# Sums over the partitions taken by GpSimd in place of matmuls of ones, and inverse roots computed on VectorE in place of GpSimd

## The chip, the cores and the metric

The kernel runs on one core of a Trainium2 chip. The metric is device time in microseconds (us) of one execution, as the median of several runs. The engines of the core are TensorE (PE, with its weight loads shown apart as PEld), VectorE (DVE), ScalarE (ACT), GpSimd (POOL) and SyncE (SP), which issues the loads and stores. Each takes its instructions in order and waits on semaphores that others raise.

## The reference, cut to what matters

```python
def rmsnorm(x, g):                       # mean over the 1024 columns
    return x * rsqrt(mean(x * x) + 1e-6) * g

def adaln(x, g, shift, scale):
    return rmsnorm(x, g) * (1 + scale[:, None, :]) + shift[:, None, :]

c_act = silu(c)                          # (1, 1024)
for i in range(2):
    mod = (c_act @ mod_w[i] + mod_b[i]).reshape(B, 3, 3, 1024)   # (shift, scale, gate) of 3 sublayers
    h = adaln(x, norm_g[i, 0], mod[:, 0, 0], mod[:, 0, 1])
    x = x + 0.5 * mod[:, 0, 2] * swiglu(h, ffn_w_in[i, 0], ffn_w_out[i, 0])
    h = adaln(x, norm_g[i, 1], mod[:, 1, 0], mod[:, 1, 1])
    x = x + mod[:, 1, 2] * (gmlp_mixer(h) if i == 0 else moba_mixer(h))
    h = adaln(x, norm_g[i, 2], mod[:, 2, 0], mod[:, 2, 1])
    x = x + 0.5 * mod[:, 2, 2] * swiglu(h, ffn_w_in[i, 1], ffn_w_out[i, 1])
return rmsnorm(x, final_norm)
```

x has 256 rows of 1024 columns, in float32. The feed-forward layers are 2816 wide. Each of the six sublayers needs three modulation vectors of 1024 columns: shift (part 0), scale (part 1) and gate (part 2), 18 vectors in all, each a product of one row with a 1024 x 1024 matrix. gmlp has a further rmsnorm, of its v half.

## The kernel before, in words

x stays in two tiles of 128 rows (t = 0, 1). All large products go through `gemm` (L201): the weights are loaded in tiles of 128 rows of the contraction, two to a transfer (`raw`, three buffers); each is split into a rounded part and a remainder, by ScalarE (L179) and VectorE (L180), into a slot `hl` (eight slots); and three TensorE products of the parts (high by high, high by low, low by high) are added up for each t. The slots set how far ScalarE and VectorE run ahead of TensorE.

The modulation vectors are prepared in the background, one stage ahead. `mod_unit(i, s, part)` stands for one vector: it clears a 128x1024 tile `ma` on GpSimd (L103), SP loads the bias row into its first row (L104), and four pieces each load two rows per partition of the weights (`mw`, L112, 1 MB) and add them, times the entries of c, with two VectorE instructions (L114). What is then left is a sum over the 128 partitions, which `reduce` takes. `gemm` calls the next of these small pieces at every fourth tile of weights (`tick`; every tile or every second one in moba). Units run for 16 of the 18 vectors; the first two (shift and scale of the first sublayer) are computed in `head` in another way.

`reduce` splits the accumulator into a rounded part and a remainder in a slot of `hl` (L121 on ScalarE, L122 on VectorE), multiplies both from the left by a matrix of ones on TensorE (L132; of halves for the gates that carry the factor 0.5), four matmuls for a vector, and copies the sums, which then stand in every row, from PSUM to `bc` (L137 on ScalarE; for the scale L134 on VectorE, which adds 1 and multiplies by the norm's weights).

At the end of a sublayer `residual` adds the gated result to x (L304, L305) and `ada` prepares the next sublayer's input: x times the scale vector (L290), the row's mean square (L264 on ScalarE, L268 on VectorE), its inverse root (`inverse_root`, L273: a power of -0.5 on GpSimd), and root and shift applied (L295), then transposes (L280) and another split (L282, L283). This is done for t = 0 while TensorE still computes t = 1, and for t = 1 while TensorE begins the next product with t = 0. `inverse_root` is called 16 times: twice in `head`, ten times in `ada`, twice for gmlp's v (`rv`), twice at the end. The tile framework places the instructions in each engine's order from its own plan of their times, so that the order on an engine is not quite that of the code.

Of the kernel before, what the change touches and what calls it, by code (L numbers as in the profile page):

```python
# [10 lines left out]

F32 = mybir.dt.float32
F32R = mybir.dt.float32r
AF = mybir.ActivationFunctionType
ALU = mybir.AluOpType
AX = mybir.AxisListType
# [2 lines left out]
P = 128  # L19
D = 1024  # L20
# [35 lines left out]
def trunk(ctx: ExitStack, tc: tile.TileContext, x, c, rel_bias, mod_w, mod_b, norm_g,  # L56
          ffn_w_in, ffn_w_out, gmlp_w_in, gmlp_v_norm, gmlp_w_s, gmlp_b_s, gmlp_w_out,
          moba_w_qkv, moba_w_o, final_norm, onehot, out):
    nc = tc.nc
    const = ctx.enter_context(tc.tile_pool(name="const", bufs=1))  # L60
    pool = ctx.enter_context(tc.tile_pool(name="pool", bufs=2))
# [4 lines left out]
    def acc_bank(name):  # L66
        return psum.tile([P, 512], F32, tag="acc", name=name, bufs=6)

    def tr_bank(name):
        return psum.tile([P, 512], F32, tag="tr", name=name, bufs=2)  # L70

    def hl_slot(shape, dt, name):
        return pool.tile(shape, dt, tag="hl", name=name, bufs=8)

    def small(name, w=1):
        return stat.tile([P, w], F32, tag=f"st{w}", name=name)

    def half_tile(name):
        return pool.tile([P, 512], F32, tag="half", name=name, bufs=4)

    x_sb = [const.tile([P, D], F32, name=f"x{t}") for t in range(NT)]
# [3 lines left out]
    make_identity(nc, ident)  # L85
    ones = const.tile([P, P], F32R, name="ones")
    nc.gpsimd.memset(ones.bitcast(F32), 1.0)
    halves_ = const.tile([P, P], F32R, name="halves")
    nc.gpsimd.memset(halves_.bitcast(F32), 0.5)
    mhalf = const.tile([P, 1], F32, name="mhalf")  # L90
    nc.gpsimd.memset(mhalf, -0.5)
    nc.scalar.activation(cs, cs, AF.Silu)


    def mod_unit(i, s, part):

        col = (s * 3 + part) * D
        st = {}
        src = mod_w[i].rearrange("(p k) n -> p k n", k=KD)

        def start():
            a = pool.tile([P, D], F32, tag="macc", name=f"ma{i}{s}{part}", bufs=2)
            nc.gpsimd.memset(a, 0.0)  # L103
            nc.sync.dma_start(a[0:1, :], mod_b[i:i + 1, col:col + D])  # L104
            st["acc"] = a

        def piece(k0):
            def f():
                if k0 == 0:
                    start()  # L110
                w = pool.tile([P, 2, D], F32, tag="mraw", name=f"mw{i}{s}{part}{k0}", bufs=2)
                nc.sync.dma_start(w, src[:, k0:k0 + 2, col:col + D])  # L112
                for j in range(2):
                    nc.vector.scalar_tensor_tensor(  # L114
                        st["acc"], w[:, j, :], cs[:, k0 + j:k0 + j + 1], st["acc"],
                        op0=ALU.mult, op1=ALU.add)
            return f

        def reduce():
            hl = hl_slot([P, 2, D], F32R, f"mhl{i}{s}{part}")  # L120
            nc.scalar.copy(hl[:, 0, :], st["acc"])  # L121
            nc.vector.tensor_sub(hl[:, 1, :], st["acc"], hl[:, 0, :].bitcast(F32))  # L122
            if part == 1:
                g = pool.tile([P, 2, D], F32, tag="mraw", name=f"g{i}{s}", bufs=2)
                nc.sync.dma_start(g[:, 0, :], norm_g[i, s:s + 1, :].to_broadcast([P, D]))
            bc = pool.tile([P, D], F32, tag="bc", name=f"bc{i}{s}{part}", bufs=3)
            lhs = halves_ if part == 2 and s != 1 else ones
            for h in range(2):
                ps = tr_bank(f"mps{i}{s}{part}{h}")
                sl = slice(h * 512, h * 512 + 512)  # L130
                for j in range(2):
                    nc.tensor.matmul(ps, lhs, hl[:, j, sl], start=j == 0, stop=j == 1)  # L132
                if part == 1:
                    nc.vector.scalar_tensor_tensor(bc[:, sl], ps, 1.0, g[:, 0, sl],  # L134
                                                   op0=ALU.add, op1=ALU.mult)
                else:
                    nc.scalar.copy(bc[:, sl], ps)  # L137
            vec[i, s, part] = bc

        return [piece(k) for k in range(0, KD, 2)] + [reduce]  # L140
# [13 lines left out]
    def split_weights(src, key, kt, cols):  # L154
# [22 lines left out]
        r = raws[key]  # L177
        hl = hl_slot([P, 2, D], F32R, f"hl_{key}_{kt}")
        nc.scalar.copy(hl[:, 0, :w], r[:, kt % 2, :w])  # L179
# [74 lines left out]
    def new_hT():  # L254
        hT["hi"] = pool.tile([P, KD, S], F32R, tag="hTh", name="hTh", bufs=1)
        hT["lo"] = pool.tile([P, KD, S], F32R, tag="hTl", name="hTl", bufs=1)

    def row_rstd(t, name):

        ss = []  # L260
        for h in range(2):
            a = small(f"ss{name}{h}")
            junk = half_tile(f"junk{name}{h}")
            nc.scalar.activation(junk, x_sb[t][:, h * 512:(h + 1) * 512], AF.Square,  # L264
                                 scale=1.0 / 32.0, accum_out=a)
            ss.append(a)
        m = small(f"m{name}")
        nc.vector.scalar_tensor_tensor(m, ss[0], EPS, ss[1], op0=ALU.add, op1=ALU.add)  # L268
        return inverse_root(m, name)

    def inverse_root(m, name):
        r = small(f"r{name}")
        nc.gpsimd.tensor_tensor(r, m, mhalf, op=ALU.pow)  # L273
        return r

    def to_columns(src, hi, lo, name):
# [23 lines left out]
    def residual(i, s, t, ps):  # L300
        for h in range(2):
            sl = slice(h * 512, h * 512 + 512)
            y = half_tile(f"y{i}{s}{t}{h}")
            nc.vector.tensor_mul(y, ps[t, h], vec[i, s, 2][:, sl])  # L304
            nc.vector.tensor_add(x_sb[t][:, sl], x_sb[t][:, sl], y)  # L305

    order = [(i, s) for i in range(2) for s in range(3)]
    fin = {}
# [48 lines left out]
    def project(i, s, src, a, lead=LEAD, early=0):  # L357

        ps = {}

        def first():
            residual(i, s, 0, ps)
            after(i, s, 0)
        yield from gemm(src, f"o{i}{s}", two(0, D), act_lhs(a), ps, lead_last=lead,
                        early=early, after_first=first)
        n = order.index((i, s)) + 1
        if n < len(order):
            prefetch(*firsts[order[n]], 3)
        residual(i, s, 1, ps)
        after(i, s, 1)  # L370
# [23 lines left out]
    def ffn_gate(g, n, w):  # L394
        sg = {}
        for t in range(NT):
            for h in range(2):
                sg[t, h] = pool.tile([P, 512], F32, tag="sg", name=f"sg{t}{h}", bufs=4)
                nc.scalar.activation(sg[t, h][:, :w], g[t, h][:, :w], AF.Silu)
        return sg  # L400
# [136 lines left out]
    def gmlp(i, s):  # L537
# [25 lines left out]
        for n in range(3):  # L563
# [7 lines left out]
            for t in range(NT):  # L571
                for h in range(2):
                    nc.scalar.activation(v[n][:, t, h * 512:(h + 1) * 512], g[t, h], AF.Gelu)
            for t in range(NT):
                for h in range(2):
                    dst = v[n][:, t, h * 512:(h + 1) * 512]
                    junk = half_tile(f"vj{t}{h}")
                    nc.scalar.activation(junk, dst, AF.Square,
                                         accum_out=ss[t][:, 2 * n + h:2 * n + h + 1])
        rv = []  # L580
        for t in range(NT):
            tot = small(f"vt{t}")
            nc.vector.reduce_sum(tot, ss[t], axis=AX.X)
            nc.vector.tensor_scalar(tot, tot, 1.0 / GM, EPS, op0=ALU.mult, op1=ALU.add)
            rv.append(inverse_root(tot, f"v{t}"))
# [9 lines left out]
        for n in range(3):  # L595
            u = product(w_in, f"gu{n}", two(n * D, D), h_lhs, lead_last=2)
            for t in range(NT):
                for h in range(2):
                    ug = pool.tile([P, 512], F32, tag="sg", name=f"ug{t}{h}", bufs=4)
                    nc.scalar.activation(ug, u[t, h], AF.Gelu)  # L600
                    sv = acc_bank(f"sv{n}{t}{h}")
# [213 lines left out]
```

## Time and profile before

| what | value |
| --- | --- |
| median of 3 runs | 1154.1 us (1153.22 to 1155.09) |
| profiled execution, its own time | 1154.63 us |
| its span in the trace | 1152.6 us |
| TensorE busy | 1127.5 us (98%) |
| VectorE busy | 827.9 us (72%) |
| ScalarE busy | 591.3 us (51%) |
| GpSimd busy | 32.2 us (3%) |
| mean granted TensorE clock | 0.996 of full speed |

The shares of busy time are of the whole span. A busy TensorE is not the same as one at its peak, because matmuls overlap and their ends are modelled; the mean duration of one matmul is longer than the spacing of two. Times in the rows below are in us from the span's start unless they are marked as ns.

### The profile page before, as it was taken

To read this page: it belongs to the slowest core of one execution; us is meant where nothing else is said; L and a number is where in the kernel's file an instruction comes from. 1 tells how busy PE (TensorE), PEld (TensorE's weight loads), DVE (VectorE), ACT (ScalarE), POOL (GpSimd) and SP (SyncE) were. 2 spreads that over 40 slices of the span, in tenths; PEclk is the share of its full clock that TensorE was granted. 3 is DMA by queue.
4 is the path that set the end of the run, shared out by engine and by line. 5 is a ranking of instruction groups with operands and counts; after the bars stand their busy time and mean duration, and the time that the engine had idled before them with its cause. 6 is when DMAs were issued, how large, how long until landed. Compare 5 with 4: busy or idle time off the path is not lost.

```text
span 1152.6 us, 14008 instructions
## 1 busy us (share of the span) xinstructions
PE 1127.5 (98%) x5381; PEld 944.6 (82%) x5381; DVE 827.9 (72%) x1008; ACT 591.3 (51%) x849; POOL 32.2 (3%) x42
## 2 busy tenths in 40 slices
PE   6999999999999999999999999999999999999997
PEld 4788998887878887888988788898877778889985
DVE  3887787845798788694678858577888878544653
ACT  3356464437555554654544546354457566544541
POOL 0000000010000000000000000000000000000000
PEclk8999999999999999999999999999999999999999
DMA  9787897657688685775779558487877555555640
GB/s 337 265 333 289 278 336 288 230 165 248 228 331 290 253 322 204 280 260 178 272 269 340 177 203 307 142 309 270 304 249 281 202 183 193 172 178 153 218 145 37
DMA packets 86538, 279.99 MB, mean 243 GB/s; under 512 B 4980, under 2 KB 15284, under 8 KB 86472
## 3 DMA queue, kind: packets, MB, share of 16 engines
q1 hardware_dynamic: 86472, 279.10, 68.4%
q8 instruction: 42, 0.69, 0.2%
q14 instruction: 24, 0.20, 0.1%
HBM read 278.01 MB, written 1.07 MB: 242 GB/s over the span
## 4 chain that ended last, share of the span: by engine, by line
PE 86%; DVE 7%; DMA 3%; ACT 2%; issue 1%; POOL 1%; SPq 0%; POOLq 0%; DVEq 0%; ACTq 0%
PE ps_o L201 27%; PE ps_g L201 19%; PE ps_u L201 19%; PE ps_v L201 5%; PE ps_gu L201 4%; PE ps_qk L201 3%; DMA mw<-in_mod_w_dram 2%; PE ta L386 2%; PE mps L132 1%; PE hps L465 1%; DVE ma L114 1%; DVE hl_g L180 1%; PE ps_u00a L201 1%; PE ps_u00b L201 1%; PE sv L609 1%
## 5 line engine op out<-in xcount | busy, mean ns | idle before, releaser
L201 PE MATMUL ps_o<-hl_o,ahl 128*128 128x512 f32 x1440 | 334.1, 391 | 1.2 <-ACT ahl L342 1.2
L201 PEld LDWEIGHTS ps_o<-hl_o,ahl 128*128 128x128 f32 x1440 | 269.0, 188 | 56.4 <-ACT ahl L342 1.4
L201 PE MATMUL ps_g<-hl_g,hTh 128*128 128x512 f32 (+1 forms) x768 | 204.1, 376 | 0.7 <-ACT hTh L498 0.7
L180 DVE TENSOR_TENSOR hl_o<-raw_o,hl_o 128x1024 fp32r<-128x1024 f32 x120 | 146.0, 1223 | 52.5 <-ACT hl_o L179 51.7
L179 ACT CAST hl_o<-raw_o 128x1024 fp32r<-128x1024 f32 x120 | 125.7, 1054 | 112.8 <-PE ps_o L201 72.6
L201 PE MATMUL ps_u<-hl_u,hTh 128*128 128x512 f32 (+1 forms) x704 | 181.5, 369 | 0.0
L114 DVE SCALAR_TENSOR_TENSOR ma<-mw,cs,ma 128x1024 f32<-128x1024 f32 x128 | 163.9, 1280 | 13.0 <-DMA mw<-in_mod_w_dram 12.3
L201 PEld LDWEIGHTS ps_g<-hl_g,hTh 128*128 128x128 f32 x768 | 142.0, 189 | 22.2 <-ACT hTh L498 1.4
L180 DVE TENSOR_TENSOR hl_g<-raw_g,hl_g 128x1024 fp32r<-128x1024 f32 (+1 forms) x96 | 107.7, 1133 | 57.9 <-ACT hl_g L179 57.6
L179 ACT CAST hl_g<-raw_g 128x1024 fp32r<-128x1024 f32 (+1 forms) x96 | 92.1, 982 | 101.8 <-PE ps_u L201 88.3
L201 PEld LDWEIGHTS ps_u<-hl_u,hTh 128*128 128x128 f32 x704 | 129.7, 188 | 17.5
L180 DVE TENSOR_TENSOR hl_u<-raw_u,hl_u 128x1024 fp32r<-128x1024 f32 (+1 forms) x88 | 98.5, 1127 | 61.9 <-ACT hl_u L179 61.0
L201 PE MATMUL ps_g<-hl_g,hTl 128*128 128x512 f32 (+1 forms) x384 | 121.2, 376 | 0.0
L179 ACT CAST hl_u<-raw_u 128x1024 fp32r<-128x1024 f32 (+1 forms) x88 | 85.6, 975 | 61.0 <-PE ps_g L201 56.1
L201 PE MATMUL ps_u<-hl_u,hTl 128*128 128x512 f32 (+1 forms) x352 | 108.6, 369 | 0.0
L201 PEld LDWEIGHTS ps_g<-hl_g,hTl 128*128 128x128 f32 x384 | 71.2, 189 | 11.1 <-issue 1.3
L201 PEld LDWEIGHTS ps_u<-hl_u,hTl 128*128 128x128 f32 x352 | 65.4, 188 | 8.7
L201 PE MATMUL ps_gu<-hl_gu,hTh 128*128 128x512 f32 x192 | 55.0, 394 | 0.0
L201 PE MATMUL ps_v<-hl_v,hTh 128*128 128x512 f32 x192 | 54.2, 392 | 0.3 <-ACT hl_v L179 0.3
L180 DVE TENSOR_TENSOR hl_v<-raw_v,hl_v 128x1024 fp32r<-128x1024 f32 x24 | 28.9, 1222 | 27.3 <-ACT hl_v L179 27.3
L201 PEld LDWEIGHTS ps_v<-hl_v,hTh 128*128 128x128 f32 x192 | 35.8, 188 | 8.2 <-ACT hl_v L179 0.5
L201 PEld LDWEIGHTS ps_gu<-hl_gu,hTh 128*128 128x128 f32 x192 | 35.8, 188 | 7.1
(160 smaller groups left out, 1204.3 us busy)
## 6 DMA issues: line engine op xcount, KB each, us to landing
mw<-in_mod_w_dram SPq DMA_DIRECT2D x64, 1024.0 KB
raw_o<-in_ffn_w_out_dram SPq DMA_DIRECT2D x44, 1024.0 KB
raw_g<-in_ffn_w_in_dram SPq DMA_DIRECT2D x32, 1024.0 KB
raw_u<-in_ffn_w_in_dram SPq DMA_DIRECT2D x28, 1024.0 KB
raw_g<-in_ffn_w_in_dram SPq DMA_DIRECT2D x16, 768.0 KB
raw_u<-in_ffn_w_in_dram SPq DMA_DIRECT2D x16, 768.0 KB
raw_v<-in_gmlp_w_in_dram SPq DMA_DIRECT2D x12, 1024.0 KB
raw_gu<-in_gmlp_w_in_dram SPq DMA_DIRECT2D x12, 1024.0 KB
```

What stands on the lines that cost most here:

```text
L114: nc.vector.scalar_tensor_tensor(st["acc"], w[:, j, :], cs[:, k0 + j:k0 + j + 1], st["acc"], op0=ALU.mult, op1=ALU.add)
L132: nc.tensor.matmul(ps, lhs, hl[:, j, sl], start=j == 0, stop=j == 1)
L179: nc.scalar.copy(hl[:, 0, :w], r[:, kt % 2, :w])
L180: nc.vector.tensor_sub(hl[:, 1, :w], r[:, kt % 2, :w], hl[:, 0, :w].bitcast(F32))
L201: nc.tensor.matmul(ps[t, h][:, :cw], lhs(k, t)[p], hls[k][:, wp, o:o + cw], start=k == 0 and p == 0 and wp == 0, stop=k == nk - 1 and p == 1)
L386: nc.tensor.transpose(ps[:, j * P:(j + 1) * P], src[:, j * P:(j + 1) * P], ident)
L465: nc.tensor.matmul(ps[part], cb[:, k, :], w[:, k, :], start=False, stop=k == KD - 1)
L609: nc.tensor.matmul(sv[:, sl], wsT[:, g, :], v[n][:, t, lo - n * D:hi - n * D], start=True, stop=True)
```

## The change

`reduce` no longer uses TensorE: one GpSimd instruction sums the accumulator over the partitions and leaves the sum in every row of `bc`; for the scale, one VectorE instruction over 1024 columns adds 1 and multiplies by the norm's weights. The factor 0.5 moves from the matrix of halves into `residual`. `inverse_root` no longer uses GpSimd: VectorE makes a first guess from the bits of the number and improves it by three of Newton's steps, eight instructions on a 128x1 tile.

```diff
@@ def reduce
-            hl = hl_slot([P, 2, D], F32R, f"mhl{i}{s}{part}")
-            nc.scalar.copy(hl[:, 0, :], st["acc"])
-            nc.vector.tensor_sub(hl[:, 1, :], st["acc"], hl[:, 0, :].bitcast(F32))
+            bc = pool.tile([P, D], F32, tag="bc", name=f"bc{i}{s}{part}", bufs=3)
+            nc.gpsimd.partition_all_reduce(bc, st["acc"], P, ReduceOp.add)
             if part == 1:
                 g = pool.tile([P, 2, D], F32, tag="mraw", name=f"g{i}{s}", bufs=2)
                 nc.sync.dma_start(g[:, 0, :], norm_g[i, s:s + 1, :].to_broadcast([P, D]))
-            bc = pool.tile([P, D], F32, tag="bc", name=f"bc{i}{s}{part}", bufs=3)
-            lhs = halves_ if part == 2 and s != 1 else ones
-            for h in range(2):
-                ps = tr_bank(f"mps{i}{s}{part}{h}")
-                sl = slice(h * 512, h * 512 + 512)
-                for j in range(2):
-                    nc.tensor.matmul(ps, lhs, hl[:, j, sl], start=j == 0, stop=j == 1)
-                if part == 1:
-                    nc.vector.scalar_tensor_tensor(bc[:, sl], ps, 1.0, g[:, 0, sl],
-                                                   op0=ALU.add, op1=ALU.mult)
-                else:
-                    nc.scalar.copy(bc[:, sl], ps)
+                nc.vector.scalar_tensor_tensor(bc, bc, 1.0, g[:, 0, :],
+                                               op0=ALU.add, op1=ALU.mult)
@@ def inverse_root
-        r = small(f"r{name}")
-        nc.gpsimd.tensor_tensor(r, m, mhalf, op=ALU.pow)
+        r, mh, t = (small(f"{a}{name}") for a in ("r", "mh", "rt"))
+        nc.vector.tensor_scalar(r.bitcast(I32), m.bitcast(I32), -0.5, float(0x5F3759DF),
+                                op0=ALU.mult, op1=ALU.add)
+        nc.vector.tensor_scalar_mul(mh, m, -0.5)
+        for _ in range(3):
+            nc.vector.scalar_tensor_tensor(t, r, mh, r, op0=ALU.mult, op1=ALU.mult)
+            nc.vector.scalar_tensor_tensor(r, t, 1.5, r, op0=ALU.add, op1=ALU.mult)
         return r
@@ def residual
-            nc.vector.tensor_add(x_sb[t][:, sl], x_sb[t][:, sl], y)
+            nc.vector.scalar_tensor_tensor(x_sb[t][:, sl], y, 0.5 if s != 1 else 1.0,
+                                           x_sb[t][:, sl], op0=ALU.mult, op1=ALU.add)
```

The tiles `halves` and `mhalf` and their fills go too.

## Rows read from the trace of the kernel before

**Rows 1.** The page's first part: busy us, share of the span, instructions of an engine.

```profile
PE 1127.5 (98%) x5381; PEld 944.6 (82%) x5381; DVE 827.9 (72%) x1008; ACT 591.3 (51%) x849; POOL 32.2 (3%) x42
```

**Rows 2.** Busy time by stretch, two whole sublayers' parts: the gmlp's output product, and moba.

```profile
core 0: us, PE busy (x) PEld busy (x) DVE busy (x) ACT busy (x) POOL busy (x), PEclk, DMA share, GB/s
...
386.00:449.00 63.00, 63.00 (x282) 52.01 (x280) 52.33 (x54) 28.79 (x37) 1.50 (x2) 1.00 0.80 301
...
832.00:932.00 100.00, 96.70 (x517) 75.40 (x516) 87.03 (x181) 66.65 (x142) 2.68 (x4) 1.00 0.66 231
```

**Rows 3.** Waits over the span: engine, line, releaser, total us, times, longest us.

```profile
ACT hl_o L179 <- PE ps_o L201: 72.6, 54, 1.7
...
PE tr_h L280 <- DVE h L295: 2.9, 7, 0.6
```

**Rows 4.** Groups of instructions by line and shape: the reduce's.

```profile
L122 DVE TENSOR_TENSOR mhl<-ma,mhl 128x1024 fp32r<-128x1024 f32 x16 | 19.6, 1224 | 12.5 <-ACT mhl L121 12.5
...
L121 ACT CAST mhl<-ma 128x1024 fp32r<-128x1024 f32 x16 | 16.9, 1054 | 15.2 <-PE ps_u L201 5.0 <-PE ps_o L201 3.4 <-issue 2.5
...
L132 PE MATMUL mps<-mhl,ones 128*128 128x512 f32 x48 | 13.3, 394 | 0.0
...
L137 ACT COPY bc<-mps 128x512 f32<-128x512 f32 x22 | 11.8, 584 | 1.7 <-PE mps L132 1.6
...
L134 DVE SCALAR_TENSOR_TENSOR bc<-mps,g 128x512 f32<-128x512 f32 x10 | 6.4, 684 | 0.6 <-PE mps L132 0.6
...
L132 PE MATMUL mps<-mhl,halves 128*128 128x512 f32 x16 | 4.3, 393 | 0.0
```

**Rows 5.** The chain that ended last, in order: start, us, what; first and last reduce.

```profile
114.12 0.93 PE mps L132 x4
...
1012.11 0.93 PE mps L132 x4
```

**Rows 6.** Groups by line and shape: GpSimd's full tiles and the roots.

```profile
L103 POOL MEMSET ma<- 128x1024 f32 x16 | 15.3, 956 | 611.7 <-DVE mhl L122 558.4 <-PE hps L477 43.7 <-DVE mx L268 9.7
...
L273 POOL TENSOR_TENSOR rx<-mx,mhalf 128x1 f32<-128x1 f32 x12 | 10.8, 902 | 288.2 <-DVE mx L268 288.2
...
L545 POOL TENSOR_SCALAR_AFFINE_SELECT ws<-ws 128x2048 f32<-128x2048 f32 x1 | 2.0, 2014 | 11.8 <-DMA ws<-in_gmlp_w_s_dram 11.8
```

**Rows 7.** Timeline of VectorE: two dependent 128x1 instructions. Start, us, instruction.

```profile
303.60 0.15 DVE L583 TENSOR_REDUCE vt<-vss 128x1 f32<-128x6 f32 x1
303.79 0.15 DVE L584 TENSOR_SCALAR vt<-vt 128x1 f32<-128x1 f32 x1
```

**Rows 8.** Timelines of VectorE and GpSimd around the root of t = 1.

```profile
456.95 0.15 DVE L268 SCALAR_TENSOR_TENSOR mx<-ssx,ssx 128x1 f32<-128x1 f32 x1
457.02 1.22 DVE L180 TENSOR_TENSOR hl_g<-raw_g,hl_g 128x1024 fp32r<-128x1024 f32 x1
458.68 1.42 DVE L295 SCALAR_TENSOR_TENSOR h<-h,rx,bc 128x512 f32<-128x512 f32 x2 [0.44 <-POOL rx L273]
...
457.25 1.40 POOL L273 TENSOR_TENSOR rx<-mx,mhalf 128x1 f32<-128x1 f32 x1 [9.55 <-DVE mx L268]
```

**Rows 9.** The same views around the root of t = 0, ten us earlier.

```profile
446.84 0.15 DVE L268 SCALAR_TENSOR_TENSOR mx<-ssx,ssx 128x1 f32<-128x1 f32 x1
...
447.72 1.42 DVE L295 SCALAR_TENSOR_TENSOR h<-h,rx,bc 128x512 f32<-128x512 f32 x2
...
447.14 0.55 POOL L273 TENSOR_TENSOR rx<-mx,mhalf 128x1 f32<-128x1 f32 x1 [45.59 <-DVE mx L268]
```

**Rows 10.** Busy time by stretch, cut at the starts of L122; columns as in Rows 2.

```profile
99.30:995.00 895.70, 887.97 (x4283) 745.15 (x4282) 673.35 (x810) 474.88 (x681) 27.04 (x27) 1.00 0.71 253
...
150.80:202.80 52.00, 52.00 (x254) 45.17 (x253) 41.55 (x41) 27.55 (x33) 0.96 (x1) 1.00 0.84 305
...
840.50:857.50 17.00, 16.67 (x77) 13.19 (x76) 16.14 (x18) 8.60 (x10) 1.55 (x2) 1.00 0.65 208
857.50:896.70 39.20, 39.14 (x203) 30.35 (x201) 31.74 (x77) 27.46 (x61) 0.96 (x1) 1.00 0.78 281
```

**Rows 11.** Waits of SP's queue of transfers.

```profile
SPq L104 <- POOL ma L103: 40.1, 11, 6.4
```

More of the change, by code (lines that the diff above doesn't have):

```diff
@@ L9 @@
 from concourse._compat import with_exitstack
+from concourse.bass_isa import ReduceOp
 from concourse.masks import make_identity
@@ L13 @@
 F32R = mybir.dt.float32r
+I32 = mybir.dt.int32
 AF = mybir.ActivationFunctionType
@@ L87, in trunk @@
     nc.gpsimd.memset(ones.bitcast(F32), 1.0)
[L88 to L91, printed above, removed]
     nc.scalar.activation(cs, cs, AF.Silu)
```

## The prediction

> **What bounds the kernel now.** I read the page's first part first, then the stretches, the waits and the chain that ended last. The reader is to see that TensorE is busy for 1127.5 of 1152.6 us, so 25 us of idle time is all that it has [rows 1], and that it stays so inside a feed-forward product: 63.00 of 63.00 us at full clock, while VectorE fills 52.3 [rows 2]. ScalarE waits for TensorE to release slots (72.6 us on one line alone), so the two engines that prepare weights run ahead [rows 3]. The one place where others come near is moba: VectorE is busy for 87.0 of 100 us and TensorE loses 3.3 [rows 2]. So whatever leaves TensorE's queue comes off the end, unless VectorE, which feeds it, falls behind by more than it is ahead. That is the whole question, because GpSimd, almost idle now [rows 1], takes on the sums.
>
> **The change part by part.** The matmuls of ones: 16 vectors by 4, 64 matmuls [rows 4]. Their mean of 394 ns overlaps the next one; their price is the piece in the chain, 0.93 us for four, and 14 of the 16 vectors stand there as such a piece, the first and the last alike [rows 5]. 16 x 0.93 = 14.9 us come off TensorE. The other two lie in moba, where TensorE is nearly full too [rows 2], so I take all sixteen.
>
> The rest of the old reduce: 16 x 1.05 us of casts and 22 x 0.58 us of copies leave ScalarE, 16 x 1.22 us of subtractions leave VectorE; for the five scale vectors 10 x 0.68 us become five instructions of the L114 kind over 1024 columns, about the same sum [rows 4]. ScalarE is half idle and VectorE a quarter [rows 1], so this is worth nothing by itself where TensorE is full; VectorE's 1.2 us a vector count below. The residual's add keeps its shape and its two inputs, so I cost it at nothing: cover is not needed, since no row of work is added. The `hl` slot that the old reduce held until TensorE reached it comes free, which lets the weights run ahead by one more; I count nothing for it.
>
> The roots: 16 powers on GpSimd become 16 x 8 small instructions on VectorE. Two dependent ones start 0.19 us apart [rows 7], so a root takes 8 x 0.195 = 1.56 us. For t = 0 the old way from the end of the mean square (446.99) to L295 (447.72) took 0.73 us [rows 9]: 0.85 us later. Five such places stand ahead of transposes for which TensorE already waits at seven of ten [rows 3]; the roots before average 902 ns against the 0.55 us of this one [rows 6, 9], so at two of the five I allow 0.5 us only. 3 x 0.85 + 2 x 0.5 = 3.6 us. For t = 1 the old way took 458.68 - 457.10 = 1.58 us [rows 8], so the new one is equal, if the 1.22 us splitting of weights that ran in its shadow is placed behind it; the split has TensorE's work on t = 0 as cover. If it is put ahead, each of five places costs up to 1.2 us, 6 us in all. The gmlp's root and the last one of the kernel pay 0.9 us each. Together 5.4 us, bounds 0.9 (only the end) and 11.4.
>
> The sum over the partitions: the trace has no such instruction. From below, a pass in which GpSimd reads and writes a tile takes 2.01 us for 2048 columns, so 1.0 us for 1024 [rows 6]. From above, a routine for every column on its own: the undisturbed power takes 0.55 us for one column [rows 9], 563 us for 1024. The nearest row is the pass, which has the same shape of work; but one pass cannot add rows to each other, and halving 128 rows takes seven, with one more to hand the sum to all rows. Eight passes are 7.9 us, an estimate; 10 to 20 us are as easy to believe.
>
> What does VectorE do meanwhile? The reader is to see in [rows 8] that the power of t = 1 starts at 457.25 and ends at 458.65, 0.41 us after VectorE's subtraction of two SBUF tiles (457.02 to 458.24), though the same power takes 0.55 us alone [rows 9]. GpSimd's read waited for VectorE's instruction to end. I take it that VectorE's instructions with two SBUF inputs wait for GpSimd in the same way, for the whole of the sum; these are L180, L114, L290, L295 and L305, and everything behind them in the queue.
>
> [...]
>
> So the price of a sum of T us is what VectorE's idle time cannot take up. Between the starts of L122, VectorE is idle for 0.9 us in the stretch from 840.5, 7.5 in the next, 10.5 in that from 150.8 [rows 10], more than 10 us in most others; each gains the 1.2 us of L122. With T = 7.9 only the first is short, by 7.9 - 0.9 - 1.2 = 5.8 us. It lies at the start of moba, where t = 1's input is being made, so there is little lead to hide it. Where the idle time suffices, the lead of eight slots is cover; without it each of 16 sums would cost up to 7.9 us.
>
> GpSimd's own queue: the clearing of the next accumulator (0.96 us) stands behind a sum, and SP waits for it before the bias row and all loads behind that; SP waited there for 40.1 us already, at most 6.4 at a time [rows 11]. T later is still less than the lead of the three raw buffers at T = 8; nothing counted, up to 5 us if it is not.
>
> Sum: 1154.6 - 14.9 + 5.4 + 5.8 = 1150.9 us for the profiled execution's own time (span 1152.6 and 2.0 around it), which stood 0.5 us above the median of the runs; so 1150.4, and I say 1150.
>
> **The rivals.** First, no holding: GpSimd takes its columns between VectorE's. For it speaks that it is fed from a long tile and not from one column; against it the row of [rows 8]. Then the 5.8 us go: 1145, whatever T is up to some 15 us.
>
> Second, on the other side: the sum is longer, 10 to 18 us, and holds VectorE. Break-even is T = 10: the two stretches of moba are then short by 7.9 and 1.3 us, together 9.2, which is the gain of 14.9 - 5.4 = 9.5. VectorE is idle for 895.7 - 673.4 = 222 us over 15 stretches, 14.8 each [rows 10]; from there on it is the bound everywhere, so T = 20 costs at least 15 x 5.2 = 78 us. On the line between, 7 us for each us, T = 13 gives 1166 and T = 16 gives 1187. For it speaks that nothing on the page shows GpSimd working across rows cheaply; against it the 1 ns a column of its passes [rows 6].
>
> Third, a routine that goes column by column with far more work, T = 40: 15 x (40 - 14.8) = 378 us on top of 1145, so 1523, and TensorE starved in every stage. [...]
>
> **How the numbers follow.** Forecast (T up to 9, VectorE held): 0.33, 1143 to 1153 with the bounds of the roots. No holding: 0.22, 1139 to 1150. Longer sum that holds: 0.30, 1153 to 1200. Column by column: 0.12. SP or a late vector at a sublayer's end by some us with a small T: 0.03, slower. A change within 0.2% (2.3 us) is about what a measurement of this kernel cannot tell from none: that takes 0.10 of the forecast, 0.01 of the second case and 0.02 of the third. Faster: 0.23 + 0.21 = 0.44. Same: 0.13. Slower: 0.28 + 0.12 + 0.03 = 0.43. The range runs from 1139, the no-holding case with no cost for the roots, to 1195; what is left out is the column case and the end of the long sum, 0.17, and 0.02 below. The likeliest case's own range is 1143 to 1153.
>
> **What would show it.** Right: no L132 in TensorE's rows and its busy time down by some 15 us; GpSimd's sums at 5 to 10 us each; VectorE's two-input instructions waiting during a sum and not its reads of PSUM; the two stretches at the start of moba longer by some 6 us; L295 of t = 0 later by 0.9 us. Wrong: sums above 10 us, with VectorE idle for as long, and TensorE waiting for L180 or L295 in every stage; or VectorE going on during the sums, which gives 1145.

## The result and the profile after

The changed kernel takes 1207.5 us (1205.6 to 1208.5 in four runs) against 1154.6 (1153.2 to 1155.3): a ratio of 1.047, 95% interval 1.046 to 1.048. It is 53 us slower, where 1150 was forecast, and lies above the range's upper end of 1195.

The page after the change, its busy line and the sum's group (busy us, mean ns, then GpSimd's idle time ahead of it and what ended most of that):

```profile
PE 1139.2 (94%) x5317; PEld 945.2 (78%) x5317; DVE 883.1 (73%) x1115; ACT 565.8 (47%) x811; POOL 126.2 (10%) x40
...
L119 POOL PARTITION_ALL_REDUCE bc<-ma x16 | 107.3, 6707 | 813.9 <-DVE y L297 529.0
```

The 64 matmuls are gone (5381 before [rows 1]), but TensorE is busy for longer, part of the time at a lower clock (below). A sum takes 6.7 us, a little less than the 7.9 that the prediction took. What it didn't see is the end of the line: of GpSimd's 813.9 us of idle time ahead of the sums, 529.0 end at `y`, L297, which is the last reader of a gate's `bc` buffer, at the end of a sublayer.

Waits of TensorE, the same view as [rows 3] (total us, times, longest):

```profile
PE ps_g L188 <- DVE hl_g L167: 16.7, 5, 3.9
PE tr_h L273 <- DVE h L288: 13.1, 5, 4.1
...
PE ps_qk L188 <- DVE hl_qk L167: 7.0, 2, 3.9
PE sv L603 <- DVE gp L605: 5.0, 3, 3.4
```

Before, `tr_h` waited 2.9 us in all [rows 3], `sv` 1.8, and the other two not at all. Busy time by stretch, columns as in [rows 2], at the ends of four sublayers:

```profile
460.00:500.00 40.00, 31.40 (x122) 23.98 (x121) 37.71 (x40) 17.70 (x24) 14.29 (x4) 0.83 0.45 163
660.00:705.00 45.00, 34.93 (x133) 25.40 (x132) 40.65 (x53) 16.62 (x24) 14.29 (x4) 0.89 0.42 146
865.00:925.00 60.00, 48.91 (x219) 37.57 (x218) 56.22 (x75) 26.39 (x42) 20.40 (x5) 0.94 0.57 194
1005.00:1050.00 45.00, 41.94 (x175) 33.76 (x174) 31.73 (x37) 21.50 (x27) 6.11 (x1) 0.92 0.57 194
```

In the same stretches before, TensorE was busy for 40.00, 45.00, 59.83 and 45.00 us at a granted clock of 1.00. Now it is idle for 33 us of 190, and its mean granted clock falls to 0.83 to 0.94. In the first stretch it is 0.50 from 474 to 484 us, around waits that end at 472.56 and 478.10 (3.07 and 3.64 us), and 1.00 from 460 to 472. Between them little changes: from 500 to 660 us it is busy for 158.5 of 160 us at 1.00. The loss stands at the sublayers' ends. GpSimd there:

```profile
465.08 6.12 POOL L119 PARTITION_ALL_REDUCE bc<-ma  x1 [79.79 <-DVE y L297]
471.26 0.95 POOL L101 MEMSET ma<- 128x1024 f32 x1
472.18 6.30 POOL L119 PARTITION_ALL_REDUCE bc<-ma  x1
```

And VectorE in the same 21 us (start, us, instruction):

```profile
465.50 4.66 DVE L298 SCALAR_TENSOR_TENSOR x<-y,x 128x512 f32<-128x512 f32 x1
...
472.43 4.49 DVE L255 SCALAR_TENSOR_TENSOR mx<-ssx,ssx 128x1 f32<-128x1 f32 x1
476.84 1.21 DVE L167 TENSOR_TENSOR hl_g<-raw_g,hl_g 128x1024 fp32r<-128x1024 f32 x1
477.97 0.14 DVE L261 TENSOR_SCALAR rx<-mx 128x1 int32<-128x1 int32 x1
...
479.23 0.21 DVE L265 SCALAR_TENSOR_TENSOR rtx<-rx,mhx 128x1 f32<-128x1 f32 x1
479.36 1.21 DVE L167 TENSOR_TENSOR hl_g<-raw_g,hl_g 128x1024 fp32r<-128x1024 f32 x1
480.49 0.15 DVE L266 SCALAR_TENSOR_TENSOR rx<-rtx,rx 128x1 f32<-128x1 f32 x1
480.56 1.27 DVE L112 SCALAR_TENSOR_TENSOR ma<-mw,cs,ma 128x1024 f32<-128x1024 f32 x1
...
485.91 1.42 DVE L288 SCALAR_TENSOR_TENSOR h<-h,rx,bc 128x512 f32<-128x512 f32 x2
```

Two things are to be seen. An instruction of 0.69 us takes 4.66 and one of 0.15 us takes 4.49, each begun within half a microsecond of a sum's start: VectorE is held for some 4 us. And between the dependent steps of a root (L261 to L266) stand instructions of 1.2 us, so that the second tile's `h` begins 9.0 us after VectorE is free of the sum (476.92 to 485.91), where 1.58 us lay between mean square and `h` before [rows 8]. Two sums stand like this at the end of each of three sublayers, single ones at 231.84 and 1006.31. VectorE beside the first of these single sums (231.84 to 238.32) shows which instructions are held: one that reads PSUM and one SBUF tile keeps its 0.68 us, the next one, with two SBUF inputs, takes 4.42.

```profile
232.26 0.68 DVE L276 TENSOR_TENSOR hTl<-tr_h,hTh 128x512 fp32r<-128x512 f32 x1
232.86 4.42 DVE L298 SCALAR_TENSOR_TENSOR x<-y,x 128x512 f32<-128x512 f32 x1
```

### The profile page after: what moved, and what is told of

The parts are those of the page before. It is cut to its first block, busy times and chain, and to the rows that moved or that the text cites. A ratio compares the mean times of both kernels' runs of the same rounds, so it can differ in the third digit from the quotient of the medians.

```text
span 1206.5 us, 13947 instructions
## 1 busy us (share of the span) xinstructions
PE 1139.2 (94%) x5317; PEld 945.2 (78%) x5317; DVE 883.1 (73%) x1115; ACT 565.8 (47%) x811; POOL 126.2 (10%) x40
## 4 chain that ended last, share of the span: by engine, by line
PE 64%; DVE 17%; DMA 8%; issue 5%; POOL 3%; ACT 2%; SPq 0%; DVEq 0%; ACTq 0%; POOLq 0%
PE ps_o L188 21%; PE ps_g L188 15%; PE ps_u L188 11%; DMA mw<-in_mod_w_dram 6%; PE ps_v L188 5%; DVE ma L112 4%; PE ps_gu L188 3%; POOL bc L119 3%; DVE hl_g L167 2%; DVE x L298 2%; PE ta L380 2%; PE hps L459 1%; PE ps_vv L188 1%; DVE hl_u L167 1%; PE ps_u00a L188 1%
## 5 line engine op out<-in xcount | busy, mean ns | idle before, releaser
L188 PE MATMUL ps_g<-hl_g,hTh 128*128 128x512 f32 (+1 forms) x768 | 213.6, 390 | 18.2 <-DVE hl_g L167 16.7
L119 POOL PARTITION_ALL_REDUCE bc<-ma x16 | 107.3, 6707 | 813.9 <-DVE y L297 529.0
L112 DVE SCALAR_TENSOR_TENSOR ma<-mw,cs,ma 128x1024 f32<-128x1024 f32 x128 | 168.0, 1312 | 29.3 <-DMA mw<-in_mod_w_dram 25.0
L188 PEld LDWEIGHTS ps_g<-hl_g,hTh 128*128 128x128 f32 x768 | 146.1, 196 | 45.3 <-DVE hl_g L167 19.1
L167 DVE TENSOR_TENSOR hl_u<-raw_u,hl_u 128x1024 fp32r<-128x1024 f32 (+1 forms) x88 | 109.2, 1257 | 53.3 <-ACT hl_u L166 52.4
L188 PE MATMUL ps_g<-hl_g,hTl 128*128 128x512 f32 (+1 forms) x384 | 125.4, 388 | 0.0
L188 PEld LDWEIGHTS ps_g<-hl_g,hTl 128*128 128x128 f32 x384 | 74.0, 196 | 12.4 <-issue 1.0
L393 ACT ACTIVATE sg<-ps_g 128x512 f32<-128x512 f32 (+1 forms) x48 | 26.7, 561 | 48.4 <-PE ps_g L188 48.1
```

The source lines that it names most:

```text
L112: nc.vector.scalar_tensor_tensor(st["acc"], w[:, j, :], cs[:, k0 + j:k0 + j + 1], st["acc"], op0=ALU.mult, op1=ALU.add)
L119: nc.gpsimd.partition_all_reduce(bc, st["acc"], P, ReduceOp.add)
L167: nc.vector.tensor_sub(hl[:, 1, :w], r[:, kt % 2, :w], hl[:, 0, :w].bitcast(F32))
L188: nc.tensor.matmul(ps[t, h][:, :cw], lhs(k, t)[p], hls[k][:, wp, o:o + cw], start=k == 0 and p == 0 and wp == 0, stop=k == nk - 1 and p == 1)
```

## The experiments

Times are medians, beside the kernel before on the same chip (1152.2 to 1154.3 us).

**The terms one by one.** First Newton's roots alone, all eight instructions put into the kernel before; the matmuls of ones stay:

```diff
-        r = small(f"r{name}")
-        nc.gpsimd.tensor_tensor(r, m, mhalf, op=ALU.pow)
+        r, mh, t = (small(f"{a}{name}") for a in ("r", "mh", "rt"))
...
+            nc.vector.scalar_tensor_tensor(r, t, 1.5, r, op0=ALU.add, op1=ALU.mult)
```

> The kernel before with one part of the change: inverse roots by Newton's steps on VectorE, the sums over the partitions still by matmuls. Theory A (the sums hold VectorE at the ends of the sublayers, where they now run two at a time, and that is nearly all of the loss): the roots cost what the prediction said, some 5 us, so 1157 to 1162. Theory B (the eight dependent steps of a root are stretched, because long instructions stand between them in VectorE's order: from the mean square to its use 9 us for t = 1 in the changed kernel against 1.6 before, at five places): 25 to 35 us, so 1180 to 1190.

Measured 1172.0 us (ratio 1.0137, 1.0106 to 1.0169), between the two: the roots cost 17.6 us. TensorE waits 13.9 us in five places for the first tile's `h`. Timeline of VectorE at one of them:

```profile
643.06 0.15 DVE L267 SCALAR_TENSOR_TENSOR mx<-ssx,ssx 128x1 f32<-128x1 f32 x1
...
644.19 1.22 DVE L179 TENSOR_TENSOR hl_g<-raw_g,hl_g 128x1024 fp32r<-128x1024 f32 x1
...
646.67 0.68 DVE L308 TENSOR_TENSOR y<-ps_o,bc 128x512 f32<-128x512 f32 x1
...
649.87 1.41 DVE L299 SCALAR_TENSOR_TENSOR h<-h,rx,bc 128x512 f32<-128x512 f32 x2
```

6.8 us from mean square to `h` (0.88 in [rows 9]), nearly all of it other tiles' work. Next, the sums alone (the changed kernel with the power back on GpSimd):

> The changed kernel with the inverse roots put back as powers on GpSimd, behind the sums in its queue. Theory A: little is won, 1195 to 1205, or it is lost again where a power waits for a sum of 6 us at a sublayer's end. Theory B: the 25 to 35 us come back, 1172 to 1182.

Measured 1220.7 us (1.0562, 1.0535 to 1.0589): slower than the whole change, which neither theory has; GpSimd's timeline at the end of this section says why. Then the roots' steps at a higher priority in the changed kernel:

> The changed kernel with the eight steps of each root given priority in the plan of VectorE's order, so that they stand close together; nothing else is changed. Theory A: at most 5 us better, 1200 to 1207. Theory B: 20 to 30 us better, 1177 to 1187, and L288 for t = 1 comes within 3 us of the mean square.

Measured 1207.1 us (1.0461, 1.0427 to 1.0495), but the steps stand apart as before (476.54 to 485.54), so it tells nothing. Next, sums that read nothing large: each replaced by a copy of one column and seven fills of `bc`, the sums left out.

```diff
-            nc.gpsimd.partition_all_reduce(bc, st["acc"], P, ReduceOp.add)
+            nc.gpsimd.tensor_copy(bc[:, 0:1], st["acc"][:, 0:1])
+            for _ in range(7):
+                nc.gpsimd.memset(bc[:, 1:], 0.25)
```

> The changed kernel with each sum replaced by GpSimd work of about its length that only writes: one column of the accumulator is copied, then the rest of the result is filled seven times (7 x 0.95 us). It leaves the sums out. Theory A, the holding by reads: VectorE's instructions keep their own lengths beside it, and 25 to 33 us come back (four or so for each sum that stands at a sublayer's end), 1174 to 1182. Theory B: the time stays within 10 us of the changed kernel, 1197 to 1207.

Measured 1160.5 us (1.0046, 1.0029 to 1.0063). GpSimd is busy for 135.7 us, more than with the sums, in the same place and with the roots' steps as far apart; 47 us of the changed kernel's time go, more than the 25 to 33 of theory A. VectorE beside the fills:

```profile
452.58 0.15 DVE L257 SCALAR_TENSOR_TENSOR mx<-ssx,ssx 128x1 f32<-128x1 f32 x1
452.65 1.21 DVE L169 TENSOR_TENSOR hl_g<-raw_g,hl_g 128x1024 fp32r<-128x1024 f32 x1
```

and GpSimd in that time:

```profile
452.64 9.89 POOL L121 MEMSET bc<- 128x1023 f32 x11
```

The split keeps its 1.21 us. So in these runs it is GpSimd's reading that holds VectorE, and not only the sum's: in the changed kernel a split takes 2.79 us instead of 1.23 where GpSimd passes over a tile that it reads and writes.

```profile
251.66 2.85 POOL L539 TENSOR_SCALAR_AFFINE_SELECT ws<-ws 128x2048 f32<-128x2048 f32 x1 [12.34 <-DMA gam<-in_gmlp_v_norm_dram]
...
252.80 2.79 DVE L167 TENSOR_TENSOR hl_v<-raw_v,hl_v 128x1024 fp32r<-128x1024 f32 x1 [0.16 <-ACT hl_v L166]
```

Last, the kernel before without its matmuls of ones (their result replaced by the first split part):

> The kernel before without its 64 matmuls of ones: the sums over the partitions are left out (the vectors are made from the first split part instead), the roots stay on GpSimd. Theory A (the matmuls' 14.9 us stand on the path, as the prediction's first term has it): 1138 to 1142 us. Rival B (they fill time in which TensorE waits anyway, or what follows takes it back): 1148 to 1155 us.

Measured 1136.8 us (0.9847, 0.9827 to 0.9868): 17.1 us below the kernel before, theory A and a little beyond, as 14.9 were predicted.

**The order of the roots' steps.** In the kernel before with Newton's roots, everything that VectorE does next was queued behind a root's last step; then the same in the changed kernel; then that with the sums taken from a copy in an `hl` slot, which need no `bc` buffer to start:

> The kernel before with Newton's roots on VectorE (matmuls of ones kept), as in the first experiment, but what VectorE does next is queued behind a root's last step, so that the eight instructions of a root stand together. Theory A (the roots' 17 us come from the 0.7 to 1.3 us instructions that the plan puts between the dependent steps, 3 to 6 of them in ten of the twelve roots): a root takes about 1.3 us from its first instruction to its last, and the time is 1152 to 1160 us. Rival B (VectorE has no room for the roots where they stand, whatever the order: the weight splits that now stand behind them come late instead): 1166 to 1176 us, as with the steps spread out.

> The changed kernel with each root's eight instructions kept together on VectorE as in the run before, the sums on GpSimd as they are. Theory A (spread-out steps and held sums cost apart from each other): 12 to 17 us below the changed kernel, 1190 to 1196 us. Rival B (what waits behind VectorE at a sublayer's end is the held stretch itself, and the steps only fill it): 1203 to 1210 us.

> The run before the last one but with each GpSimd sum taken from a copy in an hl slot and written back into the accumulator, and copied from there into bc by ScalarE, so that a sum waits for no bc buffer and stands in the middle of a sublayer. Theory A (the sums cost 47 us because five of them, and those behind them, wait for a bc buffer until the sublayer's end, where TensorE waits for VectorE; elsewhere VectorE's idle time takes the 4 us up): 1140 to 1165 us. Rival B (each of the sixteen holds VectorE for 4 us and TensorE waits for it wherever they stand): 1185 to 1200 us.

Measured 1199.6 (1.0394, 1.0372 to 1.0416), 1210.8 (1.0475, 1.0450 to 1.0500) and 1224.5 us (1.0605, 1.0585 to 1.0625). The first and the third lie above both theories, the second at the upper end of rival B's range. The edit did more than it should: the weight splits that used to run ahead of a root came behind it too, and TensorE now waits up to 5.7 us at a time for `hl_g`, `hl_v` and `hl_qk` (the third also has a wait of ScalarE, shown below for the run without that order). The lesson is rival B's: the work between the steps is needed at that moment. So only the instructions that stood between the first tile's steps were moved; `behind` queues what VectorE gets in its block after that root's last step, `residual_` is the old `residual` (`y` and `x`):

```diff
+        with behind(kt >= 2 and any(key == f[1] for f in firsts.values())):
+            nc.vector.tensor_sub(hl[:, 1, :w], r[:, kt % 2, :w], hl[:, 0, :w].bitcast(F32))
...
+        with behind(t == 1):
+            residual_(i, s, t, ps)
```

> The kernel before with Newton's roots on VectorE again (matmuls of ones kept). This time only the instructions that stood between the steps of the first tile's roots (y, x and h of the second tile, and the third and later weight splits of the next sublayer) are queued behind that root's last step; all other splits may run ahead as before, and the second tile's roots keep three to five splits between their steps. Theory A (what TensorE waits for is the first tile's h, 13.9 us in five places, because of what stands between those steps): 1152 to 1160 us. Rival B (the roots cost VectorE's time, and the splits are late instead): 1166 to 1180 us.

Measured 1159.8 us (1.0043, 1.0030 to 1.0057): theory A. TensorE waits 2.9 us for `tr_h`, as before. VectorE, same view as above:

```profile
642.12 0.16 DVE L273 SCALAR_TENSOR_TENSOR mx<-ssx,ssx 128x1 f32<-128x1 f32 x1
642.31 0.15 DVE L278 TENSOR_SCALAR rx<-mx 128x1 int32<-128x1 int32 x1
...
643.72 0.16 DVE L283 SCALAR_TENSOR_TENSOR rx<-rtx,rx 128x1 f32<-128x1 f32 x1
...
644.39 0.74 DVE L307 SCALAR_TENSOR_TENSOR h<-h,rx,bc 128x512 f32<-128x512 f32 x1
```

The eight steps take 1.57 us (642.31 to 643.88), and the roots 5.9 us in all. The prediction's 8 x 0.195 and its 5.4 us hold, for this order alone.

**The place of the sums.** This order in the changed kernel, with the accumulations (L112) of the next vector queued behind the second tile's root as well:

> The changed kernel with the same ordering of VectorE (first tile's steps together) and, as the accumulations of the next modulation vector stood between the second tile's steps, these too queued behind that root. The sums on GpSimd are as in the changed kernel, with their waits for a bc buffer. Theory A (the sums' holding at the sublayers' ends is most of the loss, the spread steps some 15 us of it): 1188 to 1197 us. Rival B (the order of the steps doesn't matter while a sum holds the engine): 1202 to 1210 us.

Measured 1167.3 us (1.0114, 1.0098 to 1.0130), far below either theory: 40 us given back. Two edits at once, so each was run alone:

> The changed kernel with only the first half of the ordering that gave 1167 us: the steps of the first tile's roots together, the accumulations left to the plan, so that sums still meet the sublayers' ends. Theory A (the 40 us that the ordering gave back come for the larger part from the sums, which the accumulations behind the second root move some 25 us past the sublayer's end): 1188 to 1200 us. Rival B (they come for the larger part from the first tile's roots, whose steps a held VectorE spreads): 1168 to 1182 us.

> The other half alone: the accumulations queued behind the second tile's root, which moves the sums past the sublayer's end, with y and x of the second tile still between the first root's steps. Theory A: 1167 to 1182 us. Rival B: 1188 to 1200 us.

Measured 1213.8 us for the roots' order alone (1.0523, 1.0492 to 1.0553) and 1169.1 us for the accumulations alone (1.0142, 1.0122 to 1.0162), whose edit is this, with `end1` the last step of the second tile's root (or of the root of gmlp's v):

```diff
-                background.pop(0)()
+                with nullcontext() if end1[0] is None else tc.issue_after(end1[0]):
+                    background.pop(0)()
```

Theory A: the accumulations' place is worth 38 us, the roots' order, with the sums at the sublayers' ends, nothing. GpSimd now starts that sum some 25 us later, when its accumulation ends and not when `bc` comes free:

```profile
489.66 6.11 POOL L119 PARTITION_ALL_REDUCE bc<-ma  x1 [108.48 <-DVE ma L112]
```

VectorE is held there too:

```profile
489.91 8.77 DVE L170 TENSOR_TENSOR hl_g<-raw_g,hl_g 128x1024 fp32r<-128x1024 f32 x4 [0.35 <-ACT hl_g L169]
```

Four splits of 1.21 us take 8.77, some 4 us more, and TensorE doesn't notice: weights are ready ahead, and it is busy for 39.45 of 40 us from 460 to 500 and 158.58 of 160 from 500 to 660, at 1.00. Is the new order good for any kernel of this shape? The same edit in the kernel before (queued behind `h` of the second tile):

> The kernel before with one edit: the accumulations of the modulation vectors queued behind h of the second tile, as in the run that gave 1169 us. Theory A (the edit's 38 us came from moving held VectorE away from the sublayers' ends; without a sum on GpSimd there is nothing to move): 1151 to 1158 us. Rival B (the order of the accumulations was wrong in any case): 1135 to 1150 us.

Measured 1163.6 us (1.0090, 1.0074 to 1.0107): slower, which neither theory has. TensorE waits once for 8.2 us with a matmul of ones for `mhl`, which is most of the loss; without that wait it would be some 1155.4 us, an estimate, so the order by itself gains nothing in this kernel. In the changed kernel some 10 of the 40 us come back where no sum holds VectorE at all (the fills under "What is left"); the other 30 are held stretches that moved.

What decides, in these runs, is not how idle VectorE is on average, but what its next instructions feed: `h` and the first splits at a sublayer's end, splits with a lead behind it. A third place was meant to test this further. Sums from a copy in an `hl` slot, written back to the accumulator and copied to `bc` by ScalarE, without and with the ordering above:

> The changed kernel with each sum taken from a copy in an hl slot, written back into the accumulator and copied into bc by ScalarE, so that no sum waits for a bc buffer; VectorE's order is left to the plan, and the roots' steps are spread as in the changed kernel. Theory A (the sums' cost of some 47 us is that of their place at the sublayers' ends): 1160 to 1180 us. Rival B (sixteen held stretches of 4 us cost the same anywhere): 1200 to 1215 us.

> Both: the sums in the middle of the sublayers, as in the run before, and the steps of the first tile's roots together with the accumulations behind the second tile's roots. Theory A (two separate causes, each mended): 1145 to 1165 us, near or below the kernel before. Rival B (holding costs the same anywhere): 1185 to 1200 us.

Measured 1224.9 (1.0623, 1.0597 to 1.0649) and 1195.3 us (1.0351, 1.0333 to 1.0369): above rival B's range and within it. But these runs don't test the place alone, since the edit brings a wait of its own. Waits in the first of them:

```profile
PE ta L385 <- DVE pr L403: 22.6, 9, 4.5
PE tr_h L278 <- DVE h L293: 20.6, 5, 7.2
...
ACT bc L129 <- POOL ma L120: 59.3, 10, 6.6
```

ScalarE and VectorE at the sum that GpSimd makes from 517.63 to 523.74:

```profile
523.78 1.05 ACT L129 COPY bc<-ma 128x1024 f32<-128x1024 f32 x1 [6.24 <-POOL ma L120]
524.73 3.88 ACT L171 CAST hl_g<-raw_g 128x1024 fp32r<-128x1024 f32 x4
...
525.86 1.23 DVE L172 TENSOR_TENSOR hl_g<-raw_g,hl_g 128x1024 fp32r<-128x1024 f32 x1 [9.78 <-POOL ma L101]
```

The copy into `bc` is ScalarE's next instruction, so ScalarE stands still until the sum has ended and casts no weights. VectorE isn't held here but idle for 9.78 us: its next split needs such a cast, the first of the four above (the row names GpSimd's fill, which ended at the same time). Behind that split stands `pr`, the gated product that a transpose needs at once, and TensorE waits 3.13 us for it at 527.74; the sum at 719.87 is followed by the same 3.13 us at 729.98. So in these places the cost is ScalarE's wait, and whether VectorE held in the middle of a sublayer costs less than at its end stays open.

**What is left.** The ordered version of 1167.3 us with the fills in place of the sums (sums left out):

> The ordered version that gave 1167 us, with each sum replaced by a copy of one column and seven fills of bc on GpSimd (0.95 us each): GpSimd is busy about as long but reads nothing large, and the sums are left out. Theory A (the terms add up: 1153.9 less 17.1 for the matmuls, as measured without them, plus 5.9 for the roots, as measured in order; what is left of the changed kernel's time is held VectorE): 1140 to 1147 us. Rival B (queuing the accumulations late, or the wait for bc, costs by itself): 1152 to 1165 us.

Measured 1150.6 us (0.9970, 0.9952 to 0.9988), between the two. Held stretches still cost 1167.3 - 1150.6 = 16.7 us, against 47 in the plan's order, so 30 of the 40 us are held time; the ordering also takes the version with the fills from 1160.5 to 1150.6, 10 us in which no sum holds VectorE. The measured terms give 1153.9 - 17.1 + 5.9 = 1142.7, so 8 us stay open. They needn't come with the order: with the fills in the plan's order 6 stay open as well (1160.5 against 1154.3 - 17.1 + 17.6 = 1154.8). With the last four sums made by TensorE again:

> The ordered version that gave 1167 us, with the four sums that stand at or after the start of moba (from 867 us on) made by the matmuls of ones again and the other twelve left on GpSimd. Theory A (8 us of TensorE's idle time and some 4 us of its lower clock stand in the stretch 865 to 925 us, so that half of the 25 us left is that stretch): 1155 to 1161 us, four times 1 us for the matmuls taken off. Rival B (the 25 us are spread over all sixteen): 1163 to 1168 us.

Measured 1165.6 us (1.0114, 1.0094 to 1.0134): in rival B's range. TensorE is busy for 59.99 of 60 us from 865 to 925 again (51.74 with the sums there), but for 153.37 instead of 158.97 from 705 to 865, where a matmul of ones now waits 4.5 us for `mhl`. So moba's start did cost 8 us, and this way to mend it costs most of that elsewhere. No version that computes all of it beat the kernel before; even without reads the order gains only 3 us.

**Why the sums alone were slowest.** GpSimd's timeline there, sums and powers on one engine:

```profile
462.83 6.45 POOL L121 PARTITION_ALL_REDUCE bc<-ma  x1 [7.12 <-DVE y L294]
...
470.28 6.80 POOL L121 PARTITION_ALL_REDUCE bc<-ma  x1
477.14 0.95 POOL L103 MEMSET ma<- 128x1024 f32 x1
487.03 0.59 POOL L263 TENSOR_TENSOR rx<-mx,mhalf 128x1 f32<-128x1 f32 x1 [8.94 <-issue]
```

The sum's 7.12 us are a wait for `y`, but 8.94 us pass ahead of the root in which GpSimd waits for nothing that the trace shows; its mean square was there at 475.52. VectorE's `h` waits 28.0 us in all for such roots, 4.5 in the kernel before. To test whether the gap belongs to the first power behind a sum, an unused one was put behind each sum, with the accumulations queued behind `h` of the second tile:

```diff
-            nc.gpsimd.partition_all_reduce(bc, st["acc"], P, ReduceOp.add)
+            ar = nc.gpsimd.partition_all_reduce(bc, st["acc"], P, ReduceOp.add)
+            with tc.issue_after(ar.ins):
+                nc.gpsimd.tensor_tensor(idle, one1, mhalf, op=ALU.pow)
```

> The sums on GpSimd with the roots on GpSimd too (as in the second experiment, 1220.7 us), the accumulations queued behind h of the second tile, and right behind each sum one more instruction: a power of one column of constants on GpSimd, whose result nobody reads. Theory A (the gaps of 7 to 9 us ahead of a root that follows a sum are GpSimd's change from the sum's code to the power's; the idle power takes it in the middle of a sublayer): no gap ahead of the roots, and with the sums moved as well 1150 to 1165 us. Rival B (the gap is something else): gaps of 7 to 9 us ahead of the roots as before, and 1175 to 1195 us.

Measured 1164.8 us (1.0102, 1.0085 to 1.0119): theory A, by the time and by where the gaps stand.

```profile
481.51 6.13 POOL L124 PARTITION_ALL_REDUCE bc<-ma  x1 [23.10 <-DVE ma L117]
495.61 0.59 POOL L126 TENSOR_TENSOR idle<-one,mhalf 128x1 f32<-128x1 f32 x1 [7.97 <-issue]
...
634.99 0.56 POOL L271 TENSOR_TENSOR rx<-mx,mhalf 128x1 f32<-128x1 f32 x1 [69.55 <-DVE mx L265]
```

The gap has moved to the unused power, in the middle of a sublayer, and the roots start as soon as their mean square is there: `h` waits 5.6 us in all for them. How much of the 56 us between the two runs (1220.7 and 1164.8) is the gap's and how much the accumulations' new place, which alone gave 38 in the changed kernel, was not separated.

## Why the prediction was wrong

**The step that failed** is "Where the idle time suffices, the lead of eight slots is cover", with the places on which it was worked out, the starts of L122. The mechanism was right: VectorE's instructions with two SBUF inputs wait while GpSimd sums (beside the 6.12 us from 465.08 one takes 4.66 instead of 0.69, and ends 1.04 us before the sum), and 7.9 us for a sum was near 6.7. But it gave 5.8 us for one short stretch, and held stretches cost 1207.5 - 1160.5 = 47 us. Five sums wait for `y`, three of them with a second one right behind, so they stand where the next sublayer's input is made, and there TensorE has too little lead: it waits 3.07 and 3.64 us for splits of `hl_g`, at 472.56 and 478.10. Average idle time between old places said nothing of that. The places moved because the new reduce's first instruction needs a `bc` buffer, while the old one's first step needed an `hl` slot. The seventh vector's last accumulation begins at 412.61 in the kernel before and at 413.77 in the changed one. But its sum now starts at 465.08, as soon as `y` lets `bc` go, and the old split of it stood 33 us behind the mean square of [rows 8]:

```profile
489.95 1.23 DVE L122 TENSOR_TENSOR mhl<-ma,mhl 128x1024 fp32r<-128x1024 f32 x1 [1.50 <-ACT mhl L121]
```

The prediction, which noted the free `hl` slot, counted nothing for this. With the accumulations queued behind the root that sum is back at 489.66; in the ordered version held stretches still cost 16.7 us, and TensorE loses 8 us at moba's start, where the prediction had its 5.8. That a later place gives back 38 us is shown; that `bc` alone made the early place is read from the releaser, and a version with more `bc` buffers wasn't tried.

**The roots** failed too, as a term: 5.4 us predicted, bounds 0.9 to 11.4; measured 17.6 in the plan's order and 5.9 with the first tile's steps together. The prediction feared one 1.2 us split ahead of the second tile's root; it was three to six instructions within the first tile's. Eight dependent steps leave a plan seven gaps to fill. In the changed kernel this adds little to the held stretches: their order alone gave nothing back (1213.8 us), and with the sums moved it is 1169.1 against 1167.3 us.

**The matmuls**: 14.9 predicted, 17.1 measured. **SP's queue**: nothing counted; SP waits 69.2 us for the accumulator's clearing, at most 18.8 at a time (40.1 and 6.4 in [rows 11]); what of this reaches the end was not separated.

**The sum**: -17.1 + 17.6 + 47.0 = +47.5 of 52.9 us; 5 us stay open, as with the fills alone, and so do the 8 us of the ordered version. In the prediction's own arithmetic, eight passes of 1.007 us (half of 2014 ns, [rows 6]) are 8.1 us and not 7.9, which moves its forecast by 0.2 us; and its line for T above 10 leaves out the 1.2 us of L122 that the forecast counts: with them T = 20 costs 60 us and not 78.

**The rivals.** The longer sum that holds ended on the right side, with a wrong mechanism: it needed T = 10, and 6.7 was enough. No holding and the column routine are out by the rows above. The 40 us that the column routine gave a sum stand in no row; a sum takes 6.7. VectorE's instructions with two SBUF inputs were held beside a sum, which reads its tile (4.66 us for 0.69), and not beside the fills (a split's usual 1.21 us).

## What to carry to other kernels

When work moves to another engine, ask first which buffer its first instruction now waits for: that sets its place, and the place sets the price; the same sixteen held stretches cost 47 us with eight of them at the sublayers' ends and 17 where splits run ahead. Ask the same of what then waits for the result: a copy on ScalarE kept that engine still for 59 us in ten places. A chain of tiny dependent instructions costs what a scheduler puts between them (17.6 us here, 5.9 with the first tile's steps together), so cost it by the longest neighbours and not by its own steps. Idle time is cover only if what comes next on the held engine isn't awaited.

## What the runs showed of the hardware

VectorE comes free before a sum ends: 470.16 against 471.20, and 476.92 against 478.48. An instruction of 128x1 elements is held as long as one of 128x512 (4.49 and 4.66 us). Holding goes both ways: the sum at 342.76, beside which VectorE ran three splits first (3.48 us from 342.58), took 9.28 us, the shortest 6.11.

From a sum to a power GpSimd shows nothing for 8.94 us in the sums-only run; with the unused power the gap is 6.75 to 7.98 us in twelve of sixteen places, and longer in the others. In the sums-only run its queue has 20 `MODIFY_POOL_CONFIG` at the power's line and 20 at the sums'; with the unused power 32 stand at that power's line and none at the roots'. In the changed kernel, which has no powers, the sums' line has two, at 62.1 us, ahead of the first sum, and none later. What GpSimd does in the gaps the trace does not show.
